# Scaling the first branch's operands later in ScalarE's order, and three gate tiles in the merge for one pair of weights

## The chip, the cores and the metric

The kernel runs on one core of a Trainium2 chip. The metric is the time of one execution on the device, in microseconds (us). The core has a matrix engine, TensorE (PE in the profile, with its weight loads as PEld), and three engines for elementwise work: VectorE (DVE), ScalarE (ACT) and GpSimd (POOL). SyncE (SP) issues nearly all DMA transfers. Each engine works off its own list of instructions in order and waits on semaphores for the others.

## The reference

One layer of a decoder in float32: S = 1024 positions, D = 1024, a hidden width of 4096.

```
h = rms_norm(x)
[A | B | C | nsa_gates | G0 G1 G2] = h @ W_in
y_0 = subln(diff_attention(A))            # 4 heads of 128, 512 columns
y_1 = sliding_window_attention(B)         # 8 heads of 64, window 128, sinks
y_2 = native_sparse_attention(C)          # compressed + selected + window 512
x = x + (sum_n sigmoid(G_n) * (y_n @ P_n)) @ W_out
x = x + relu(rms_norm(x) @ W_up)**2 @ W_down
```

`subln` is an RMS norm of each head's output with a gain per channel. P_n is 512 x 1024. The last step of the first line that matters here, the merge, is the sum over the three branches n.

## The kernel before

Every float32 operand of a product is kept as a high part and a remainder, `hi` and `lo`, and a product is three matmuls (`mm3`, L118 to L120: hi by hi, hi by lo, lo by hi). Making such a pair (`split`, L90 and L91) is a copy on ScalarE and a subtraction on VectorE or GpSimd. Activations are held transposed: channels on the 128 partitions, positions along the free axis, in two halves of 512 positions.

The order of TensorE's work is written out by hand. `mix` interleaves an attention stage (fine-grained steps) with a stage of plain products, its `dense` partner, so that TensorE has products to run while the softmax goes through the other engines. The order on the other engines is set at build time by a scheduler that goes by a timeline of its own, so a change in the code may move instructions on them in ways that the diff does not show. SP's transfers are issued in one order too.

The stages that matter:

- **Branch C, second half** (about 900 to 1172 us). The partner of the attention is `first_branch`. It runs over two halves of the positions. For each it projects some of the 24 merge gates (`gates(n)`; the sigmoid, L1125, goes to DRAM, `gd`), then scales the four operands of branch 0 (`scaled`), then makes the eight products of branch 0 and multiplies each by its gate (L1183). The products go to DRAM (`yd`).
- **One scaled operand**: a box `tm` of the tag "tm" (two buffers) receives branch A's output and its row of norms (L1141, L1142), GpSimd multiplies the two in place (L1145), ScalarE writes the high part `xh` times the gain (L1146), VectorE the remainder `xl` (L1147). The two buffers of the tag also hold the gates of branch 0, so the third operand's loads wait for the first operand's `xl`. `parts.pop(0)()` issues these three instructions between two steps of a gate's projection.
- **Attention on the other engines** in that stage: L715 makes scores `sc`, VectorE adds the bias and takes the row maximum `mc` (L739), ScalarE takes the exponential with the row sum (`expo`, L747), VectorE multiplies by one over the sum (L1048), TensorE transposes (`tr`, L763), ScalarE and VectorE split the transposed `p` into `ph` and `pl` (L90, L91) with GpSimd zeroing the rest of the tiles (L760, L761), and L903 and L904 accumulate `ac`; L909 and L910 take it out (`ot`, `ob`).
- **The merge** (`merge_and_mlp`, 1172 to about 1272 us). Branch 1 has eight weights and two halves, sixteen products; branch 2 has two halves and eight weights each, sixteen products. A product is twelve matmuls into one of six PSUM banks. VectorE makes g = (g + 1) x product (L1218 in branch 1, L1229 in branch 2). In branch 1 GpSimd adds g to y, which was read from `yd` (L1216, L1220). In branch 2 VectorE adds it (L1231), and the sum is split into `mh` and `ml` (L1232, L1233). A gate tile `g` is filled by a DMA from `gd` (L1154) and is free once it has been added; the pool `bg` has two of them. The weights' pairs `wh`, `wl` are taken from two pools in turn (`parts`), three pairs in each.
- After it come W_out (`wo`, L1285) and the MLP.

`GATES` divides the 24 gate projections among the stages; entries 3 and 4 are the gates before and during the scaling of the first half, entry 5 those before the scaling of the second half, and what remains of 24 those during it.

Of the kernel before, what the change touches and what calls it, by code (L numbers as in the profile page):

```python
# [13 lines left out]
AF = mybir.ActivationFunctionType  # L14
# [50 lines left out]


PACE = (1.6, 1.4144, 1.156, 1.392, 1.45, 1.7)
GATES = (2, 2, 12, 1, 4, 2)
STEP = ((1.702, 0.1048), (2.2511, 0.078), (1.85, 0.078))
DIST = 2  # L70
WR = 4
# [4 lines left out]
class Kernel:  # L76
# [27 lines left out]
    def parts(self, pool=None, bufs=None, tag="w"):  # L104
        pool = pool or self.wp
        if self.other is not None:
            self.turn += 1
            pool = self.other if self.turn % 2 else pool
        return [pool.tile([P, self.w_n], F32R, name=tag + x, tag=tag + x, bufs=bufs or self.w_bufs) for x in "hl"]

    def spare(self, k):
# [62 lines left out]
    def run(self):  # L174
# [70 lines left out]
        with tc.tile_pool(name="cp", side="right", **kw) as cp:  # L245
# [7 lines left out]
            self.mm = mm2  # L253
            self.mix(self.compress(cp, z, w1), self.gates(GATES[0]), PACE[5])
        self.alone = False
# [15 lines left out]
        self.load_bias(range(8, 12))  # L271
        self.mix(self.pipeline(self.items_b(1, st_b1), last=True), self.gates(GATES[1]), PACE[2])
        self.at.release()
# [15 lines left out]
        for g in range(2):  # L289
# [7 lines left out]
            if g == 0:  # L297
                dense = self.gates(GATES[2])
            else:
# [444 lines left out]
        return self.at.tile([P, n], F32, name="p", tag=f"p{kind}{qb % 2}", bufs=2)  # L744

    def expo(self, p, ps, m, l):
        self.nc.scalar.activation(p, ps, AF.Exp, bias=m, scale=-1.0, accum_out=l)  # L747

    def pblocks(self, blocks):

# [384 lines left out]
    def scaled(self, i, s, hi, lo):  # L1135

        nc = self.nc
        box = self.sq.tile([P, self.tm_n], F32, name="tm", tag="tm", bufs=2)
        raw, r = box[:, 0:512], box[:, 512:1024]
        row = self.rd[i]  # L1140
        nc.sync.dma_start(raw, self.od[i, :, s])  # L1141
        nc.sync.dma_start(r, bass.AP(tensor=row.tensor, offset=row.offset + s.start, ap=[[0, P], [1, 512]]))  # L1142

        def parts():
            nc.gpsimd.tensor_tensor(raw, raw, r, op=ALU.mult)  # L1145
            nc.scalar.activation(hi, raw, AF.Copy, scale=self.subln)  # L1146
            nc.vector.scalar_tensor_tensor(lo, raw, self.subln, hi.bitcast(F32), op0=ALU.mult, op1=ALU.subtract)  # L1147

        return parts
# [15 lines left out]
    def first_branch(self):  # L1165
        nc = self.nc
        for half, n, m in ((0, GATES[3], GATES[4]), (1, GATES[5], 24 - sum(GATES))):
            s = slice(half * 512, half * 512 + 512)
            yield from self.gates(n)
            o = [self.parts(tag="x") for _ in range(4)]  # L1170
            parts = [self.scaled(i, s, *o[i]) for i in range(2)]
            for k, c in enumerate(self.gates(m)):
                if k % 4 == 3 and parts:
                    parts.pop(0)()
                    if k < 8:
                        parts.append(self.scaled(2 + k // 4, s, *o[2 + k // 4]))
                yield c
            for d in range(KT):
                w = self.weight(self.a["wbr"][0, d], 512)
                g = self.gate(self.sq, "tm", 2, 0, d, s)  # L1180
                ps = self.branch(0, d, [x[0] for x in o], [x[1] for x in o], w)
                with self.tc.high_priority(offset=self.urgent):
                    nc.vector.scalar_tensor_tensor(g, g, 1.0, ps, op0=ALU.add, op1=ALU.mult)  # L1183
                nc.sync.dma_start(self.yd[d, :, s], g)
                yield 2.6

    def merge_and_mlp(self):
        tc, nc, a = self.tc, self.nc, self.a
        kw = dict(bufs=1, reuse_waits="tile")
        halves = [slice(0, 512), slice(512, 1024)]  # L1190
        mp = tc.alloc_tile_pool(name="mp", side="left", **kw)
        mh = mp.tile([P, KT, S], F32R, name="mh")
        ml = mp.tile([P, KT, S], F32R, name="ml")
        pre = tc.alloc_tile_pool(name="pre", side="right", **kw)
        self.wp = pre
        self.w_n, self.wr_bufs, self.w_bufs = 512, 3, 3
        with (tc.tile_pool(name="bb", side="right", **kw) as bb, tc.tile_pool(name="br", side="right", **kw) as br,
              tc.tile_pool(name="bl", side="left", **kw) as bl, tc.tile_pool(name="bg", side="left", **kw) as bg,
              tc.tile_pool(name="wx", side="left", **kw) as wx):
            self.other = wx  # L1200
            ob = [[bb.tile([P, S], F32R, name=f"ob{i}{x}") for x in range(2)] for i in range(4)]
            oc = [None, None]
            y = [None, None]
            for half, pool in ((0, br), (1, bl)):
                y[half] = pool.tile([P, KT, 512], F32, name="y")
                oc[half] = [[pool.tile([P, 512], F32R, name=f"oc{i}{x}") for x in range(2)] for i in range(4)]
            for s in halves:
                for i in range(4):
                    self.operand(self.od[4 + i], s, *[x[:, s] for x in ob[i]])
            for d in range(KT):  # L1210
                w = self.weight(a["wbr"][1, d], 512)
                if d == 1:
                    self.wo_after = self.last_load
                for half, s in enumerate(halves):
                    g = self.gate(bg, "g", 2, 1, d, s)
                    nc.sync.dma_start(y[half][:, d], self.yd[d, :, s])  # L1216
                    ps = self.branch(1, d, [x[0][:, s] for x in ob], [x[1][:, s] for x in ob], w)
                    nc.vector.scalar_tensor_tensor(g, g, 1.0, ps, op0=ALU.add, op1=ALU.mult)  # L1218
                    v = y[half][:, d, :]
                    nc.gpsimd.tensor_tensor(v, v, g, op=ALU.add)  # L1220
            for half, s in enumerate(halves):
                for i in range(4):
                    self.operand(self.od[8 + i], s, *oc[half][i])
            for half, s in enumerate(halves):
                for d in range(KT):
                    w = self.weight(a["wbr"][2, d], 512)
                    g = self.gate(bg, "g", 2, 2, d, s)
                    ps = self.branch(2, d, [x[0] for x in oc[half]], [x[1] for x in oc[half]], w)
                    nc.vector.scalar_tensor_tensor(g, g, 1.0, ps, op0=ALU.add, op1=ALU.mult)  # L1229
                    v = y[half][:, d, :]  # L1230
                    nc.vector.tensor_tensor(v, v, g, op=ALU.add)  # L1231
                    nc.scalar.activation(mh[:, d, s], v, AF.Copy, scale=0.5)  # L1232
                    nc.vector.scalar_tensor_tensor(ml[:, d, s], v, 0.5, mh[:, d, s].bitcast(F32),  # L1233
                                                   op0=ALU.mult, op1=ALU.subtract)

        self.tail(mp, mh, ml, halves, pre)
# [373 lines left out]
```

## Time and profile before

| quantity | value |
|---|---|
| time of the runs (3), median | 2022.37 us (2022.16 to 2026.12) |
| the profiled execution | 2024.17 us |
| its span | 2022.4 us |
| mean granted clock of TensorE | 0.982 |
| instructions of the scaled operands (POOL, ACT, DVE) | 8 each, 911.3 to 1050.7 us |
| DMA | 221.59 MB, mean 110 GB/s |

The profile describes one execution; its span runs from the first to the last instruction, and the execution's own time holds 1.8 us more. "Busy" is the share of the span in which an engine executes something. A row of the timeline has the start, the duration, the engine, the line and the operation, out<-in by the names of the program, and at its end in brackets how long its engine had stood idle before and what released it. The granted clock is the share of full speed at which TensorE ran.

### The profile page before, as it was taken

To read this page: it belongs to the slowest core of one execution; us is meant where nothing else is said; L and a number is where in the kernel's file an instruction comes from. 1 tells how busy PE (TensorE), PEld (TensorE's weight loads), DVE (VectorE), ACT (ScalarE), POOL (GpSimd) and SP (SyncE) were. 2 spreads that over 40 slices of the span, in tenths; PEclk is the share of its full clock that TensorE was granted. 3 is DMA by queue.
4 is the path that set the end of the run, shared out by engine and by line. 5 is a ranking of instruction groups with operands and counts; after the bars stand their busy time and mean duration, and the time that the engine had idled before them with its cause. 6 is when DMAs were issued, how large, how long until landed. Compare 5 with 4: busy or idle time off the path is not lost. (4 is left out here: it accounts for less than half of the span.)

```text
span 2022.4 us, 30612 instructions
## 1 busy us (share of the span) xinstructions
PE 1889.4 (93%) x9842; PEld 1618.3 (80%) x9842; DVE 1410.4 (70%) x3216; ACT 1006.0 (50%) x2550; POOL 953.8 (47%) x1138
## 2 busy tenths in 40 slices
PE   7999999998899999998989798998999998999998
PEld 6888889887688888877878686786788886888876
DVE  6747877788667677567676835648655544889898
ACT  5356555666445555445555623325454554433431
POOL 4455444643361212262232246218444545789783
PEclk9999999999999999999999998999999999999998
DMA  6132012101211111213243475425544446445343
GB/s 221 51 105 56 12 53 54 52 16 56 81 42 47 57 58 52 72 42 97 84 139 100 137 238 186 142 83 182 177 158 154 161 137 240 140 157 162 120 146 115
DMA packets 123773, 221.59 MB, mean 110 GB/s; under 512 B 14580, under 2 KB 35604, under 8 KB 123612
## 3 DMA queue, kind: packets, MB, share of 16 engines
q1 hardware_dynamic: 122028, 213.87, 32.7%
q10 hardware_dynamic: 1584, 5.77, 0.8%
q8 instruction: 78, 1.28, 0.3%
q14 instruction: 83, 0.68, 0.1%
HBM read 158.68 MB, written 64.83 MB: 111 GB/s over the span
## 5 line engine op out<-in xcount | busy, mean ns | idle before, releaser
L91 POOL TENSOR_TENSOR wl<-wr,wh 128x512 fp32r<-128x512 f32 (+3 forms) x246 | 325.6, 1330 | 273.9 <-ACT wh L90 231.2
L90 ACT ACTIVATE wh<-wr 128x512 fp32r<-128x512 f32 (+3 forms) x258 | 150.3, 590 | 185.7 <-PE mm L119 114.9
L715 PE MATMUL sc<-st 128*128 128x256 f32 (+5 forms) x736 | 182.3, 342 | 24.3 <-ACT p L747 24.0
L90 ACT ACTIVATE ph<-tr 128x384 fp32r<-128x384 f32 (+3 forms) x280 | 138.4, 497 | 116.2 <-PE tr L763 96.1
L91 DVE TENSOR_TENSOR pl<-tr,ph 128x384 fp32r<-128x384 f32 (+3 forms) x280 | 155.6, 559 | 43.6 <-ACT ph L90 41.5
L760 POOL MEMSET ph<- 128x128 f32 x152 | 34.7, 228 | 269.4 <-PE ac L903 220.8
L118 PE MATMUL mm<-hh,wh 128*128 128x512 f32 x384 | 159.4, 415 | 0.0
L715 PEld LDWEIGHTS sc<-st 128*128 128x128 f32 x736 | 122.3, 191 | 44.9 <-ACT p L747 36.0
L120 PE MATMUL mm<-hh,wl 128*128 128x512 f32 x384 | 152.1, 396 | 0.0
L119 PE MATMUL mm<-hl,wh 128*128 128x512 f32 x384 | 152.0, 396 | 0.0
L119 PE MATMUL mm<-wl,wh 128*128 128x512 f32 x352 | 140.3, 398 | 9.0 <-POOL wl L91 9.0
L118 PE MATMUL mm<-wh 128*128 128x512 f32 x352 | 140.4, 399 | 8.1 <-DVE x L1492 5.2
L90 ACT ACTIVATE wh<-u 128x512 fp32r<-128x512 f32 x162 | 93.1, 620 | 106.4 <-PE mm L119 27.9
L120 PE MATMUL mm<-wh,wl 128*128 128x512 f32 x352 | 139.5, 396 | 0.0
L763 PE MATMUL tr<-ident,p 128*128 128x128 f32 x792 | 129.9, 277 | 9.3 <-DVE st L568 8.3
L747 ACT ACTIVATE p<-sc,mc 128x256 f32<-128x256 f32 (+5 forms) x200 | 106.7, 539 | 46.8 <-DVE mc L739 43.5
L903 PE MATMUL ac<-ph,st 128*128 128x256 f32 x392 | 110.2, 299 | 20.4 <-DVE ob L910 13.7
L91 POOL TENSOR_TENSOR wl<-s,wh 128x512 fp32r<-128x512 f32 x64 | 89.1, 1399 | 78.9 <-ACT wh L90 78.9
L118 PE MATMUL mm<-wh,hh 128*128 128x384 f32 (+1 forms) x320 | 116.3, 364 | 0.6 <-ACT raw L524 0.6
L91 DVE TENSOR_TENSOR wl<-u,wh 128x512 fp32r<-128x512 f32 x98 | 113.5, 1159 | 3.6 <-ACT wh L90 3.6
L904 PE MATMUL ac<-pl,st 128*128 128x256 f32 x392 | 106.3, 291 | 7.4 <-DVE pl L91 6.7
L119 PE MATMUL mm<-wl,hh 128*128 128x384 f32 (+1 forms) x320 | 109.7, 343 | 0.0
(312 smaller groups left out, 5714.0 us busy)
## 6 DMA issues: line engine op xcount, KB each, us to landing
ud<-u SPq DMA_DIRECT2D x112, 256.0 KB, 2.1
u<-ud SPq DMA_DIRECT2D x98, 256.0 KB, 3.6
wr<-wu SPq DMA_DIRECT2D x76, 256.0 KB, 3.0
wr<-wd SPq DMA_DIRECT2D x64, 256.0 KB, 3.0
gd<-go SPq DMA_DIRECT2D x48, 256.0 KB, 2.0
g<-gd SPq DMA_DIRECT2D x48, 256.0 KB, 3.3
wr<-wg SPq DMA_DIRECT2D x40, 256.0 KB, 2.7
wr<-wbr SPq DMA_DIRECT2D x40, 256.0 KB, 3.4
```

The source lines that it names most:

```text
L90: nc.scalar.activation(hi, src, AF.Copy)
L91: (eng or nc.vector).tensor_tensor(lo, src, hi.bitcast(F32), op=ALU.subtract)
L118: mm(out, lh, rh, start=first, stop=False, skip_group_check=more)
L119: mm(out, lh, rl, start=False, stop=False, skip_group_check=more)
L120: mm(out, ll, rh, start=False, stop=last, skip_group_check=more)
L715: self.nc.tensor.matmul(ps[:, off:off + k1 - k0], q[:, t * P:(t + 1) * P], k[:, k0:k1], start=i == 0, stop=i == 1)
L747: self.nc.scalar.activation(p, ps, AF.Exp, bias=m, scale=-1.0, accum_out=l)
L760: nc.gpsimd.memset(ph[0:rows, o:o + P].bitcast(F32), 0.0)
L763: nc.tensor.transpose(pt[0:rows, o:o + P], src, self.ident)
L903: nc.tensor.matmul(ac, v, ph, start=first, stop=False)
L904: nc.tensor.matmul(ac, v, pl, start=False, stop=last)
```

## The change

There are five edits.

1. `GATES`: of the five gates that go with the scaling of the first half, two instead of one are projected ahead of it and three instead of four during it; of the three of the second half, one instead of two ahead and two instead of one during it. The totals stay.
2. In `first_branch` an operand is scaled every `gap` steps, with gap = min(4 m, 8) = 8 for both halves, where it was every 4.
3. `expo` keeps the last exponential that was issued, and `scaled` puts ScalarE's copy behind it in ScalarE's order (`issue_after`).
4. The merge's gate tiles are three instead of two, for branch 1 and for branch 2.
5. The second of the two pools of weight pairs in the merge holds two pairs instead of three.

```
-GATES = (2, 2, 12, 1, 4, 2)
+GATES = (2, 2, 12, 2, 3, 1)
...
             pool = self.other if self.turn % 2 else pool
+            bufs = bufs or (2 if pool is self.other else None)
...
     def expo(self, p, ps, m, l):
-        self.nc.scalar.activation(p, ps, AF.Exp, bias=m, scale=-1.0, accum_out=l)
+        self.last_exp = self.nc.scalar.activation(p, ps, AF.Exp, bias=m, scale=-1.0, accum_out=l).ins
...
             nc.gpsimd.tensor_tensor(raw, raw, r, op=ALU.mult)
-            nc.scalar.activation(hi, raw, AF.Copy, scale=self.subln)
+            with self.tc.issue_after(self.last_exp):
+                nc.scalar.activation(hi, raw, AF.Copy, scale=self.subln)
...
+            gap = min(4 * m, 8)
             for k, c in enumerate(self.gates(m)):
-                if k % 4 == 3 and parts:
+                if k % gap == gap - 1 and parts:
                     parts.pop(0)()
-                    if k < 8:
-                        parts.append(self.scaled(2 + k // 4, s, *o[2 + k // 4]))
+                    if k < 2 * gap:
+                        parts.append(self.scaled(2 + k // gap, s, *o[2 + k // gap]))
...
-                    g = self.gate(bg, "g", 2, 1, d, s)
+                    g = self.gate(bg, "g", 3, 1, d, s)
...
-                    g = self.gate(bg, "g", 2, 2, d, s)
+                    g = self.gate(bg, "g", 3, 2, d, s)
```

TensorE's order is the same, instruction for instruction. Line numbers behind L746 are 1 to 3 higher in the changed kernel (L747 is L748, L1146 is L1148, L1154 is L1156, L1216 is L1219).

ScalarE in the first half of `first_branch`, before: the third and fourth copy `xh` among the exponentials `p` of one block of the attention.

```order
L1146 ACTIVATE xh_11378<-tm_11450,subln_212 128x512
L90 ACTIVATE wh_11852<-wr_11851 128x512
L747 ACTIVATE p_11551,lc_11534<-sc_11536,mc_11535 128x448
L747 ACTIVATE p_11551,lc_11534<-sc_11545,mc_11535 128x320
L747 ACTIVATE p_11586,lc_11534<-sc_11570,mc_11535 128x384
L747 ACTIVATE p_11586,lc_11534<-sc_11582,mc_11535 128x256
L1146 ACTIVATE xh_11380<-tm_11506,subln_212 128x512
```

The first and second copy in the changed kernel, some 20 us of the program further on:

```order
L748 ACTIVATE p_11703,lc_11638<-sc_11699,mc_11639 128x256
L1148 ACTIVATE xh_11608<-tm_11616,subln_212 128x512
L1126 ACTIVATE go_11742<-mm_11634 128x512
L90 ACTIVATE ph_11733<-tr_11735 128x512
L90 ACTIVATE ph_11774<-tr_11776 128x384
L748 ACTIVATE p_11764,lc_11749<-sc_11751,mc_11750 128x512
L748 ACTIVATE p_11764,lc_11749<-sc_11758,mc_11750 128x512
L748 ACTIVATE pc3_7133,lc_11749<-sc_11784,mc_11750 128x64
L90 ACTIVATE wh_12147<-wr_12146 128x512
L90 ACTIVATE ph_11804<-tr_11806 128x384
L748 ACTIVATE p_11818,lc_11749<-sc_11784,mc_11750 128x384
L748 ACTIVATE p_11818,lc_11749<-sc_11814,mc_11750 128x256
```

The copies have gone from ahead of a block's exponentials to behind the last of a block; what stood behind the copies of before now has nothing of the kind ahead of it.

VectorE in the second half, before: the fourth and last remainder `xl`, ahead of the row sums `lc` and the attention's output `ob`.

```order
L739 ISA sc_12980,mc_12952<-sc_12980,bias_10690,mc_12952 128x256
L739 ISA mc_12952 128x1
L1147 SCALAR_TENSOR_TENSOR xl_13362<-tm_13475,subln_212,xh_13361 128x512
L1044 TENSOR_TENSOR lc_12951<-lc_12951 128x1
L1045 RECIPROCAL lc_12951<-lc_12951 128x3
L1046 TENSOR_TENSOR lc_12951<-lc_12951,cgate_224 128x3
L910 TENSOR_TENSOR ob_13007<-ac_12779,ot_13006 64x256
```

In the changed kernel the last remainder of that half stands some 54 us of the program later, behind the scaling of the `p` of another block (L1049) and just ahead of the merge's first operands `ob`:

```order
L1046 RECIPROCAL lc_13589<-lc_13589 128x3
L1047 TENSOR_TENSOR lc_13589<-lc_13589,cgate_224 128x3
L1049 TENSOR_SCALAR pc1_7131<-pc1_7131,lc_13589 128x64
L1049 TENSOR_SCALAR p_13597<-p_13597,lc_13589 128x256
L1049 TENSOR_SCALAR p_13636<-p_13636,lc_13589 128x256
L1149 SCALAR_TENSOR_TENSOR xl_13143<-tm_13369,subln_212,xh_13142 128x512
```

SP at the merge's start, before: the loads of `y` and of the first gates `g`.

```order
L911 DMA od<-ob 64x256 x2
L1154 DMA g<-gd 128x512 x2
L911 DMA od<-ob 64x256
L1216 DMA y<-yd 128x512 x12
L1154 DMA g<-gd 128x512
L1216 DMA y<-yd 128x512 x4
L1154 DMA g<-gd 128x512
```

In the changed kernel:

```order
L912 DMA od<-ob 64x256 x2
L1156 DMA g<-gd 128x512 x2
L912 DMA od<-ob 64x256
L1219 DMA y<-yd 128x512
L1156 DMA g<-gd 128x512
L1219 DMA y<-yd 128x512 x10
L1156 DMA g<-gd 128x512
L1219 DMA y<-yd 128x512 x4
L1156 DMA g<-gd 128x512
```

The third gate's load has moved ahead of eleven loads of `y`; the later ones each wait for the tile of three gates before instead of two.

## The prediction

> **What bounds the kernel now.** I read the page first, for the share of each engine, then TensorE's timeline for its idle time, then the table of windows around what I found, since an average over this program says little.
>
> ```profile
> span 2022.4 us, 30612 instructions
> PE 1889.4 (93%) x9842; PEld 1618.3 (80%) x9842; DVE 1410.4 (70%) x3216; ACT 1006.0 (50%) x2550; POOL 953.8 (47%) x1138
> ```
>
> TensorE (PE) is busy 93% and its order of work is written out by hand and isn't touched, so the change can only move the 7% in which it stands and the time in which its clock is low. In the windows table a row is stretch, length, then busy time of PE, PEld, DVE, ACT and POOL, then granted clock, DMA share and GB/s:
>
> ```profile
> 925.00:930.00 5.00, 3.41 (x9) 2.83 (x10) 2.61 (x11) 3.01 (x10) 2.54 (x2) 0.60 0.38 114
> 930.00:935.00 5.00, 5.00 (x25) 4.29 (x25) 2.43 (x5) 2.20 (x4) 1.56 (x3) 0.72 0.22 57
> 1030.00:1040.00 10.00, 7.94 (x49) 6.91 (x48) 6.05 (x17) 4.16 (x12) 3.15 (x6) 0.93 0.53 166
> 1040.00:1050.00 10.00, 9.57 (x48) 8.27 (x48) 7.79 (x26) 4.67 (x14) 4.11 (x5) 0.90 0.38 126
> 1172.62:1227.16 54.54, 54.54 (x240) 45.16 (x241) 20.76 (x25) 13.47 (x22) 32.06 (x25) 1.00 0.74 248
> 1227.16:1271.78 44.62, 37.44 (x145) 29.95 (x144) 29.91 (x38) 15.46 (x28) 23.29 (x17) 0.89 0.58 188
> ```
>
> The first four rows are branch C's second half, where the first branch's operands are scaled; the last two are the merge. The stalls of PE in them, with what released it in brackets:
>
> ```profile
> 914.47 0.50 PE L715 MATMUL sc<-st 128*128 128x256 f32 x2 [0.91 <-ACT p L747]
> 926.59 0.79 PE L715 MATMUL sc<-st 128*128 128x256 f32 x2 [3.77 <-ACT p L747]
> 1036.04 0.38 PE L903 MATMUL ac<-ph,st 128*128 128x256 f32 x1 [0.96 <-ACT ph L90]
> 1037.53 0.38 PE L904 MATMUL ac<-pl,st 128*128 128x256 f32 x1 [1.10 <-DVE pl L91]
> 1046.04 0.51 PE L715 MATMUL sc<-st 128*128 128x256 f32 x2 [0.43 <-ACT p L747]
> 1053.65 0.39 PE L903 MATMUL ac<-ph,vct 128*128 128x256 f32 x1 [2.40 <-DVE ob L910]
> 1233.36 0.76 PE L118 MATMUL mm<-oc,wh 128*128 128x512 f32 x1 [3.31 <-DVE g L1218]
> 1244.46 0.77 PE L118 MATMUL mm<-oc,wh 128*128 128x512 f32 x1 [3.86 <-DVE g L1229]
> ```
>
> Each of the first six stands near one of the scaled copies; each of the last two waits for a gate's product. So both parts of the change aim at stalls that PE has.
>
> **The first branch: what goes.** The chain in front of the 3.77 us stall, from the timeline of all engines:
>
> ```profile
> 922.16 0.54 DVE L91 TENSOR_TENSOR pl<-tr,ph 128x384 fp32r<-128x384 f32 x1
> 923.81 0.72 ACT L1146 ACTIVATE xh<-tm,subln 128x512 fp32r<-128x512 f32 x1 [2.02 <-POOL tm L1145]
> 924.56 0.75 DVE L1147 SCALAR_TENSOR_TENSOR xl<-tm,subln,xh 128x512 fp32r<-128x512 f32 x1 [0.51 <-ACT xh L1146]
> 925.23 0.48 DVE L739 CUSTOM_DVE_ANT_0 sc<-sc,bias,mc 128x256 f32<-128x256 f32 x1
> 925.81 0.64 ACT L747 ACTIVATE p<-sc,mc 128x448 f32<-128x448 f32 x1 [0.76 <-DVE mc L739]
> ```
>
> ScalarE (ACT) stands 2.02 us for GpSimd's product, copies, then VectorE (DVE) takes the remainder xl, and only then the score's maximum (L739) that the exponential waits for. Without the pair, L739 can follow pl at 922.70 instead of 925.23: PE would go on 2.5 us sooner, and 1.3 us of the stall stay (score, maximum and exponential in turn). At the other five stalls one copy of 0.72 or one remainder of 0.75 to 0.99 (at 1036) stands in front; I take 0.7 of 0.91, 0.7 of 0.96, 1.0 of 1.10, 0.4 of 0.43, and 0.7 of 2.40. Sum with the 2.5: 6.0 us, between 2.5 (the first chain alone) and 9.6 (all six rows).
>
> Behind these stalls the granted clock is low: 5 x 0.40 + 5 x 0.28 = 3.4 us in the first two windows, of which up to 0.8 lies in idle time already counted (1.59 us idle at half); I take 3.0. In the next two, 10 x 0.07 + 10 x 0.10 = 1.7. If the stall shrinks below what lowers the clock, these 4.7 us go. Together 10.7 us.
>
> That the clock falls behind stalls is the trace's reading: it is 0.93 and 0.90 around 1038, after 0.96 and 1.10 us of idle, and 1.00 in the merge's window without idle. [...]
>
> **The first branch: what is paid.** The eight products, copies and remainders remain, in other places:
>
> ```profile
> L1145 POOL TENSOR_TENSOR tm<-tm x8: 1264/1286/1403, 911.3 to 1048.6; 128x512 f32<-128x512 f32 x8
> L1146 ACT ACTIVATE xh<-tm,subln x8: 714/724/727, 912.7 to 1050.0; 128x512 fp32r<-128x512 f32 x8
> L1147 DVE SCALAR_TENSOR_TENSOR xl<-tm,subln,xh x8: 737/752/1306, 913.4 to 1050.7; 128x512 fp32r<-128x512 f32 x8
> 957.41 0.39 PE L904 MATMUL ac<-pl,st 128*128 128x256 f32 x1 [1.44 <-DVE pl L91]
> 1092.33 1.23 DVE L91 TENSOR_TENSOR pl<-tr,ph 128x512 fp32r<-128x512 f32 x2 [0.35 <-POOL pl L761]
> 1093.20 0.28 PE L904 MATMUL ac<-pl,st 128*128 128x256 f32 x1
> 1104.94 0.61 DVE L1048 TENSOR_SCALAR p<-p,lc 128x256 f32<-128x256 f32 x2
> 1105.03 0.39 PE L119 MATMUL mm<-xl,wh 128*128 128x512 f32 x1
> ```
>
> ScalarE's copies now stand behind exponentials that already wait for DVE, so I price them at nothing there: ACT is busy 4.2 of 10 us in these windows; uncovered, each would be 0.72. The remainders land on DVE ahead of a pl. The one near 956.7 is ahead of the pl that PE already waits 1.44 us for: +0.75. Of the next half's, the third is ahead of the pl at 1092.33, whose first half PE takes at 1093.20, some 0.2 us after it is made: +0.55. The others meet pl's with about 1 us of slack. The last remainder of the second half stands behind the two L1048 that end at 1105.55, so it ends near 1106.30, and branch 0's matmul needs it at 1105.03: +1.27. On GpSimd (POOL) a product of 1.29 us can stand ahead of the zeroing (L760, L761) of a ph that PE waits for: 0 to 1.3, I take 0.6, half, since no row shows which comes first. Moved with the copies are two pairs of loads on SP a half (the third and fourth operand, whose box is freed by xl); they come a few us later, behind nothing that waits. The gate that moves between the halves leaves PE's order as it is. Paid: 0.75 + 0.55 + 1.27 + 0.6 = 3.2 us, between 0 and 8 x 0.75 = 6.0. The first branch nets **7.5 us**.
>
> **The merge.** What holds the products is a ring of two gate tiles:
>
> ```profile
> 1225.68 0.68 DVE L1218 SCALAR_TENSOR_TENSOR g<-g,mm 128x512 f32<-128x512 f32 x1
> 1228.11 1.29 POOL L1220 TENSOR_TENSOR y<-y,g 128x512 f32<-128x512 f32 x1
> 1229.43 0.48 SPq L1154 DMA_DIRECT2D g<-gd  x1
> 1232.52 0.69 DVE L1218 SCALAR_TENSOR_TENSOR g<-g,mm 128x512 f32<-128x512 f32 x1 [6.17 <-DMA g<-gd]
> DVE g L1218 <- DMA g<-gd: 20.7, 8, 6.2
> DVE g L1229 <- DMA g<-gd: 9.3, 6, 4.0
> ```
>
> A tile is multiplied until 1226.36, added to y until 1229.40, refilled from 1229.43, and multiplied again until 1233.21: 6.85 us a round, 3.42 us a gate with two tiles. PE makes a product in 54.54 / 20 = 2.73 us (240 matmuls, 12 a product). DVE falls behind by 0.7 us a product, and when PE's six banks are full PE stands. With three tiles a gate takes 2.28 us, less than 2.73, so DVE keeps up: the ring no longer sets the pace. In the last window 144 matmuls should take 12 x 2.73 = 32.7 us and the stretch takes 44.62: 11.9 us lost, of which the two stalls are 7.2 and the low clock (0.11 x 44.62 = 4.9) about the rest. All 11.9 go if no other wait takes their place.
>
> The tile is paid with one pair of weights: six pairs in two pools become five.
>
> ```profile
> 1178.17 0.63 ACT L90 ACTIVATE wh<-wr 128x512 fp32r<-128x512 f32 x1 [2.91 <-PE mm L119]
> 1183.61 0.63 ACT L90 ACTIVATE wh<-wr 128x512 fp32r<-128x512 f32 x1 [4.81 <-PE mm L119]
> 1278.72 0.50 PE L119 MATMUL mm<-wo,mh 128*128 128x512 f32 x1 [1.79 <-DVE wo L91]
> ```
>
> A pair of the smaller pool is now rewritten after product n-4 and needed at product n: three products, 8.2 us, for a copy of 0.63 and a remainder of about 1.3. ACT already waits 2.91 and 4.81 us for such releases while PE stands nowhere (54.54 of 54.54), so this costs between nothing and one stall like 3.86; I take 1, near the row without idle. The wait for DVE's wo at 1278.72 may shorten when DVE isn't behind: 0 to 1.79, I take 0.9. The merge nets 11.9 - 1 + 0.9 = **11.8 us**.
>
> **Sum.** 7.5 + 11.8 = 19.3 us. The profiled execution took 2024.17 us (span 2022.4 and 1.8 around it), which gives 2004.9; it is 1.8 us above the median of the runs, 2022.37, and against that the forecast is 2003.
>
> **The rivals.**
> - Merge only: the moved copies, remainders and products make as much new idle as they remove, and the clock stays low there. For it: DVE is busy 6 to 8 of 10 us in those windows. Against: it asks for 10.7 us of cost where I count 3.2. 2022.4 - 11.8 = 2010.6.
> - First branch only: with three tiles DVE's product waits for something else (POOL is busy 32 of 54.5 us in the merge and adds each y; or the five weight pairs), and PE stands as long. Against: POOL's add of 1.29 per 2.73 us. 2022.4 - 7.5 = 2014.9.
> - The low clock has another cause than these stalls and stays when they go: 4.7 us in the first branch and 4.7 in the merge less, 19.3 - 9.4 = 9.9, so 2012.5. Against: in the merge's first window, as dense as any, the clock is 1.00.
> - Nothing that PE waits for moves: the copies come later, but the exponentials were waiting for score and maximum, and the gate ring for the y loads' traffic (DMA share 0.74). Then 2022.
> - Slower: the ring of five pairs. ACT works in order; a wh copy that waits for its pair holds the mh copies behind it, and PE lacks the weights. A late pair costs about what a late gate did, 11.9 / 2 = 5.95 us with its clock. It decides from four late pairs of the eight that the small pool serves in branch 2: 4 x 5.95 = 23.8 against 19.3 gained. Five would give 2022.4 + 29.8 - 19.3 = 2033. Against: 8.2 us of lead for 1.9 of work.
>
> **How the numbers follow.** Forecast 0.56, merge only 0.11, first branch only 0.10, clock stays 0.05: these are faster, 0.82. Nothing moves: 0.10, the same. Slower: 0.08. About 0.2% (4 us) is what a measurement of this kernel can tell from no change. The forecast's own bounds are a gain of 9.6 + 4.7 and 11.9 + 1.8, nothing paid, 28 us (1994), down to 2.5 + 4.7 - 6.0 and 11.9 - 3.9, 9 us (2013). The range of 1995 to 2017 takes this in, and first branch only; it leaves out the last two cases, 0.18.
>
> **What would show it.** Right: no stall near 926 above 1.5 us, and the clock over 0.95 in 925 to 935 and 1030 to 1050; a stall of about 1.3 us at branch 0's second start; in the merge no row of PE released by L1221 or L1232 (the gates' products), the window of its last 12 products near 33 us, and DVE's waits for g below 2 us each. Wrong: a PE stall released by wh or wl in branch 2 (the ring of weights), by pl beside an xl (more than 3 us in all), or the low clock in the same places without a stall before it.

## The result, and the profile after

The changed kernel takes 2006.72 us in the median of six runs (2002.73 to 2011.69); the kernel before, over six runs, 2023.56 us (2019.25 to 2027.96). The ratio is 0.9913, with a 95% interval of 0.9897 to 0.9928: 17.6 us less, between 14.6 and 20.8. The forecast was 19.3 less. A second set of runs of the same kernel, further down, gave 0.9897 (0.9878 to 0.9915).

The profiled execution of the changed kernel took 2011.07 us, so it is one of its longer ones, 13.1 us below the profiled execution of before. The first lines of its page, as before:

```profile
span 2009.3 us, 30615 instructions
PE 1889.3 (94%) x9842; PEld 1616.0 (80%) x9842; DVE 1422.2 (71%) x3216; ACT 1006.1 (50%) x2550; POOL 959.3 (48%) x1138
```

Nothing has become cheaper: the busy times of PE and ACT are within 0.1 us of before, DVE's and POOL's are a little higher. What went is idle time and low clock. The windows table, with the same columns as in the prediction (the granted clock is third from the end):

```profile
905.00:935.00 30.00, 27.78 (x160) 23.75 (x161) 24.38 (x73) 17.91 (x52) 7.52 (x13) 1.00 0.31 99
1030.00:1050.00 20.00, 18.77 (x109) 16.15 (x108) 14.43 (x52) 11.46 (x36) 5.18 (x13) 1.00 0.17 57
1168.22:1222.76 54.54, 54.54 (x241) 45.16 (x242) 23.36 (x29) 12.82 (x22) 36.19 (x27) 1.00 0.81 269
1222.76:1261.38 38.62, 34.49 (x145) 26.49 (x144) 36.12 (x38) 18.68 (x34) 25.77 (x17) 1.00 0.67 227
```

The clock is 1.00 where it was 0.60, 0.72, 0.93 and 0.90 (first two rows) and where it was 0.89 (last row). The last row runs from the same instruction of PE to the same instruction as the last window of before: 38.62 us instead of 44.62. PE's timeline has these waits in the places that the prediction named, and two further on (1109 and 1119) that the kernel before has too:

```profile
923.93 0.50 PE L716 MATMUL sc<-st 128*128 128x256 f32 x2 [1.10 <-ACT p L748]
952.08 0.39 PE L905 MATMUL ac<-pl,st 128*128 128x256 f32 x1 [1.63 <-DVE pl L91]
1031.17 0.39 PE L904 MATMUL ac<-ph,st 128*128 128x256 f32 x1 [0.33 <-POOL ph L761]
1042.83 0.39 PE L904 MATMUL ac<-ph,vct 128*128 128x256 f32 x1 [0.81 <-DVE ob L911]
1084.02 0.38 PE L905 MATMUL ac<-pl,st 128*128 128x256 f32 x1 [1.30 <-DVE pl L91]
1097.18 0.50 PE L120 MATMUL mm<-xl,wh 128*128 128x512 f32 x1 [0.81 <-DVE xl L1149]
1109.75 0.52 PE L716 MATMUL sc<-st 128*128 128x256 f32 x2 [2.08 <-ACT p L748]
1119.69 0.38 PE L904 MATMUL ac<-ph,vct 128*128 128x256 f32 x1 [1.78 <-DVE ob L911]
1223.84 0.50 PE L121 MATMUL mm<-oc,wl 128*128 128x512 f32 x1 [0.47 <-POOL wl L91]
1230.63 0.50 PE L121 MATMUL mm<-oc,wl 128*128 128x512 f32 x1 [1.01 <-POOL wl L91]
```

The 3.77 us stall is 1.10, those near 914, 1036, 1037 and 1046 are gone, and 2.40 is 0.81. Of the two long stalls behind gates none is left. New are the waits for GpSimd's zeroing (1031), for a pl (1084) and for the last operand (1097), all three foreseen, and the waits for the weights' remainders wl: the waits table of 1165 to 1275 gives their sum, and the gates':

```profile
DVE g L1221 <- DMA g<-gd: 12.5, 5, 4.0
PE mm L121 <- POOL wl L91: 4.1, 5, 1.3
DVE g L1232 <- DMA g<-gd: 0.7, 1, 0.7
```

Since PE's instructions are the same in every kernel of this study, in the same order, each can be compared by the start of the same instruction in two timelines. The table gives, for stretches between fixed instructions of PE (named by their start before), how much longer or shorter than in the profile of before each profiled execution was, in us.

| kernel | to 880 | 880 to 1020 | 1020 to 1095 | 1095 to 1172.6 | 1172.6 to 1227 | 1227 to 1272 | 1272 to 1300 | whole PE |
|---|---|---|---|---|---|---|---|---|
| the change | +0.8 | -6.1 | -3.8 | +4.7 | 0.0 | -6.0 | -2.1 | -13.2 |
| the change, second set | -4.3 | -6.6 | -3.5 | +4.5 | +1.6 | -10.3 | -2.1 | -19.5 |
| fb_only | -4.5 | -6.5 | -3.2 | +6.5 | +1.2 | -2.1 | +2.1 | -5.8 |
| merge_only | -8.5 | -2.1 | +2.2 | +0.4 | 0.0 | -7.4 | -2.1 | -17.8 |
| no_issue_after | -5.9 | -2.3 | +2.0 | +0.7 | 0.0 | -7.2 | -2.1 | -13.6 |
| gates2_pairs5 | -7.2 | -6.5 | -2.6 | +5.2 | 0.0 | -2.1 | +1.9 | -10.6 |
| no_gap | -2.2 | -2.7 | -2.9 | +7.9 | +1.6 | -7.7 | -2.1 | -6.5 |
| gap_8_6 | -5.6 | -4.0 | -3.5 | +4.9 | +1.6 | -10.2 | -2.1 | -17.8 |
| wo_later | -1.9 | -6.5 | -2.9 | +3.6 | 0.0 | -6.2 | -2.1 | -15.1 |
| wo_spread | -5.2 | -4.1 | -2.8 | +5.2 | +1.6 | -8.8 | -2.1 | -15.2 |
| wo_spread_early | -4.3 | -3.9 | -2.6 | -0.5 | 0.0 | -6.5 | -2.1 | -20.7 |
| gates3_pairs6 | -7.8 | -4.0 | -3.6 | +5.9 | +1.6 | -6.0 | +16.7 | +5.0 |
| ob_later | -4.4 | -6.7 | -3.2 | +9.1 | 0.0 | -6.8 | -2.1 | -11.9 |

The first column is a warning: no edit touches that part, and it differs by up to 9 us between executions. So a single "whole" of this table says little, and verdicts below go by the ratios of the runs; the stages are read where the change is. The column 1095 to 1172.6 holds a loss that the prediction did not have.

### The profile page after: what moved, and what is told of

The parts are those of the page before. It is cut to its first block, busy times and chain, and to the rows that moved or that the text cites. A ratio compares the mean times of both kernels' runs of the same rounds, so it can differ in the third digit from the quotient of the medians.

```text
span 2009.3 us, 30615 instructions
## 1 busy us (share of the span) xinstructions
PE 1889.3 (94%) x9842; PEld 1616.0 (80%) x9842; DVE 1422.2 (71%) x3216; ACT 1006.1 (50%) x2550; POOL 959.3 (48%) x1138
## 5 line engine op out<-in xcount | busy, mean ns | idle before, releaser
L764 PE MATMUL tr<-ident,p 128*128 128x128 f32 x792 | 129.8, 277 | 8.5 <-DVE st L569 7.0
L748 ACT ACTIVATE p<-sc,mc 128x256 f32<-128x256 f32 (+5 forms) x200 | 106.7, 539 | 50.8 <-DVE mc L740 47.5
```

The source lines that it names most:

```text
L748: self.last_exp = self.nc.scalar.activation(p, ps, AF.Exp, bias=m, scale=-1.0, accum_out=l).ins
L764: nc.tensor.transpose(pt[0:rows, o:o + P], src, self.ident)
```

## The experiments

All times are ratios to the kernel before, measured beside it on the same chip, with 95% intervals. fb_only, merge_only, no_issue_after and gates2_pairs5 share a chip; so do gates3_pairs6, gap_8_6, wo_later and no_gap; and so do whole_again, wo_spread and wo_spread_early. Kernels that share none are compared by their ratios.

### The two parts, and their pieces

`fb_only` takes back edits 4 and 5:

```
-            bufs = bufs or (2 if pool is self.other else None)
...
-                    g = self.gate(bg, "g", 3, 1, d, s)
+                    g = self.gate(bg, "g", 2, 1, d, s)
```

(and the same for branch 2.)

> The first branch's part alone (edits 1 to 3; two gate tiles and six weight pairs as before). If the two parts add up: in the profile the stalls and the low clock of 912 to 1054 gone as with the whole change (about 12 us earlier at 1053), then some 3 us given back at a pl near 1093 and at the last xl; the merge with its two stalls of 3.3 and 3.9 us and their clock; in all 4 to 10 us faster than before. Rival, the gain comes from the merge alone: within 3 us of before. Rival, the parts need each other: slower than before.

Measured: 0.9954 (0.9937 to 0.9970), 9.3 us less. The merge has its stalls as before, both somewhat shorter:

```profile
1226.55 0.70 PE L119 MATMUL mm<-oc,wh 128*128 128x512 f32 x1 [2.62 <-DVE g L1221]
1237.37 0.77 PE L119 MATMUL mm<-oc,wh 128*128 128x512 f32 x1 [3.50 <-DVE g L1232]
```

The gain stands without the merge's part. More than 3 us are given back in 1095 to 1172.6, though: +6.5 in the table.

`merge_only` is the kernel before with edits 4 and 5 alone.

> The merge's part alone (edits 4 and 5). If the parts add up: the first branch as before with its 3.77 us stall, the merge without stalls behind g, with five short ones behind wl of 4 us together, 7 to 10 us faster than before. Together with the first branch's part alone it should make the 17 us of the whole. Rival, the merge's gain hangs on the phase in which the first branch leaves the other engines: stalls behind g come back, within 3 us of before.

Measured: 0.9947 (0.9928 to 0.9966), 10.7 us less, no stall behind g, four waits behind wl of 3.0 us together. The two parts make 9.3 + 10.7 = 20.0 us; the whole makes 17.6 in its first set and 20.8 (0.9897) in its second. They add up within their intervals. Up to 1120 us of its own time the other engines of this kernel run what they ran before, in the same order, so its -2.1 and +2.2 in the table's stretches from 880 to 1095 show how much one execution differs from another there.

`no_issue_after` is the whole change without edit 3:

```
-            with self.tc.issue_after(self.last_exp):
-                nc.scalar.activation(hi, raw, AF.Copy, scale=self.subln)
+            nc.scalar.activation(hi, raw, AF.Copy, scale=self.subln)
```

> The whole change without edit 3: copies wherever the scheduler puts them, which is near their places of before, four in a row of exponentials in each half. If the rule that puts a copy behind an exponential is what removes the stall at 926: a stall of over 3 us there and low clock behind it, low clock near 1038 too, the time that of the merge's part alone, 5 to 10 us slower than the whole change. Rival, the gates and the wider gap do it: within 3 us of the whole change.

Measured: 0.9945 (0.9924 to 0.9966), as the merge's part alone. The stall is back:

```profile
919.64 0.58 PE L716 MATMUL sc<-st 128*128 128x256 f32 x1 [2.87 <-ACT p L748]
```

So edits 1 and 2 do nothing without edit 3: up to 1122 us the order on VectorE, ScalarE and GpSimd, copies included, is that of the kernel before.

`no_gap` is the whole change without edits 1 and 2 (`GATES` as before, `gap = 4`).

> The whole change without edits 1 and 2: gates and spacing as before, the copies behind the last exponential only. Two copies of the first half then stay within the block of the 3.77 us stall, each behind an exponential. If order behind the exponential alone is what counts: the stall near 926 shrinks below 1.5 us. If the distance counts too: a stall of 1.5 to 3.5 us stays there, and the time lies between the merge's part alone and the whole change, 2 to 5 us above the latter.

Measured: 0.9936 (0.9918 to 0.9954), 5 to 8 us above the whole change by the ratios of its two sets; the interval overlaps that of the first set and lies just above that of the second. Behind the exponentials, but too close together, the copies of the first half still make most of the long stall:

```profile
923.00 0.50 PE L716 MATMUL sc<-st 128*128 128x256 f32 x2 [3.25 <-ACT p L748]
```

The copies of the second half, though, stand some 45 us later than before, and the stalls near 914, 1036, 1037 and 1046 are gone here as well. So the long stall needs order and distance; for the four others the order alone was enough.

`gates2_pairs5` is the whole change with two gate tiles again (edit 4 undone, edit 5 kept).

> The whole change without edit 4: two gate tiles and five pairs of weights. If the ring of gate tiles makes the merge's long stalls: two stalls behind g of 3 to 4 us with low clock behind them, as before, and the merge 6 to 12 us longer than with three tiles. If the missing pair makes the short stalls behind wl: they stay. Rival, the earlier third gate load and the order on SP do it, not the ring: no stall behind g.

Measured: 0.9950 (0.9933 to 0.9967), the same as fb_only. Both long stalls are back in PE's timeline, and in the windows table, below it, the clock of the last twelve products is 0.92:

```profile
1222.08 0.72 PE L119 MATMUL mm<-oc,wh 128*128 128x512 f32 x1 [2.97 <-DVE g L1221]
1232.35 0.74 PE L119 MATMUL mm<-oc,wh 128*128 128x512 f32 x1 [2.91 <-DVE g L1232]
```

```profile
1215.97:1258.54 42.57, 36.69 (x145) 29.11 (x144) 29.81 (x37) 15.92 (x29) 25.78 (x18) 0.92 0.61 204
```

The ring of gate tiles made the stalls. The missing pair costs nothing here: 42.57 us against 42.56 in fb_only with six pairs, and no wait behind wl. By what I had expected, this speaks against the missing pair as the maker of the short waits behind wl; but the stalls behind the gates also leave the remainders more time. The waits show only once the gates no longer hold PE back.

### Why a pair was given up

`gates3_pairs6` is the whole change without edit 5: three gate tiles and six pairs.

> The whole change without edit 5: three gate tiles and all six pairs of weights. In SP's order all eight loads of W_out then stand behind the last weight of branch 2, since their buffers lie where the second pool of weights ends. If the pair was given up for that room: no short stall behind wl in branch 2, but PE waits for wo at W_out's first products, 10 us or more with low clock behind, and the time is above that of the whole change by 8 us or more. Rival, the ring of five pairs is what costs (the short stalls, 5.4 us): then this is up to 5 us faster than the whole change.

Measured: 1.0021 (1.0007 to 1.0035), 22 us slower than the whole change by the ratios, the largest effect of the study. Branch 2 runs without a wait, and then W_out waits for its own operands, four times:

```profile
1256.80 0.80 PE L119 MATMUL mm<-wo,mh 128*128 128x512 f32 x1 [4.66 <-ACT wo L90]
1263.77 0.80 PE L119 MATMUL mm<-wo,mh 128*128 128x512 f32 x1 [2.62 <-ACT wo L90]
1270.57 0.80 PE L119 MATMUL mm<-wo,mh 128*128 128x512 f32 x1 [2.45 <-ACT wo L90]
1277.28 0.80 PE L119 MATMUL mm<-wo,mh 128*128 128x512 f32 x1 [2.35 <-ACT wo L90]
```

The same place in the windows table:

```profile
1255.50:1282.90 27.40, 15.93 (x28) 7.95 (x29) 9.10 (x10) 9.71 (x17) 10.02 (x8) 0.50 0.50 171
```

The clock is 0.50 throughout. In SP's rows the first loads of W_out (`x<-wo`) stand behind the last weights, first this kernel, then the changed one:

```profile
1251.74 0.90 SPq L1288 DMA_DIRECT2D x<-wo  x2
```

```profile
1182.00 1.01 SPq L1288 DMA_DIRECT2D x<-wo  x2
```

This is what the theory of the room said: with the pair, the loads of W_out find no place before the last weights are used up.

### The waits behind wl

In the changed kernel's timeline of GpSimd, two halves of a row of W_out stand ahead of the remainders that PE waits for at 1223.84 and 1230.63 (an entry with x2 is two instructions):

```profile
1218.64 3.45 POOL L91 TENSOR_TENSOR wo<-x,wo 128x512 fp32r<-128x512 f32 x2
1222.05 3.44 POOL L91 TENSOR_TENSOR wl<-wr,wh 128x512 fp32r<-128x512 f32 x2
1225.45 3.44 POOL L91 TENSOR_TENSOR wo<-x,wo 128x512 fp32r<-128x512 f32 x2
1228.87 1.71 POOL L91 TENSOR_TENSOR wl<-wr,wh 128x512 fp32r<-128x512 f32 x1
```

A third of the five waits (1256.22, 0.91 us) has two such halves ahead of it as well. The other two have another chain. Ahead of the longest (1243.24, 1.27 us) GpSimd stood idle until ScalarE had made a copy `wh`, and ScalarE had waited for that weight's load:

```profile
1239.51 0.63 ACT L90 ACTIVATE wh<-wr 128x512 fp32r<-128x512 f32 x1 [2.39 <-DMA wr<-wbr]
1240.22 2.97 POOL L91 TENSOR_TENSOR wl<-wr,wh 128x512 fp32r<-128x512 f32 x2 [5.64 <-ACT wh L90]
```

GpSimd waits for a copy `wh` ahead of the one at 1249.43 (0.47 us) too. Whether the smaller ring of pairs has a part in these two is not shown: gates3_pairs6 has six pairs and none of the waits, but there W_out's loads and splits come later too.

`wo_later` holds GpSimd's splits of W_out back behind the remainder of branch 2's seventh weight:

```
...
+                with tc.issue_after(self.wl_after if k % 2 == 0 else self.wo_after):
+                    self.split(wo[k][0][:, s], wo[k][1][:, s], r[:, s], nc.vector if k % 2 else nc.gpsimd)
...
```

> The whole change with GpSimd's splits of W_out held back behind the weight of branch 2's seventh product (first half). If these splits make the first short stalls behind wl (0.47 and 1.01 us near 1224 and 1231): those two are gone, and a later one may grow, as two W_out rows are then split back to back (6.9 us); net 0 to 2 us faster in the merge. Rival, the ring of five pairs makes them: they stay.

Measured: 0.9914 (0.9894 to 0.9934), no difference to the whole change. The first two waits are gone, and behind four halves in a row (6.85 us) there is one as long as several:

```profile
1224.51 6.85 POOL L91 TENSOR_TENSOR wo<-x,wo 128x512 fp32r<-128x512 f32 x4
1231.32 3.38 POOL L91 TENSOR_TENSOR wl<-wr,wh 128x512 fp32r<-128x512 f32 x2
1234.76 0.50 PE L121 MATMUL mm<-oc,wl 128*128 128x512 f32 x1 [3.92 <-POOL wl L91]
```

So the first two waits move with W_out's splits. Two kernels spread them; both also have the second half's operands every 6 steps:

```
-            gap = min(4 * m, 8)
+            gap = 8 if half == 0 else 6
...
+                with tc.issue_after(self.los[min(6 + k + i, 15)] if k % 2 == 0 else self.wo_after):
...
```

(`los` are the remainders of branch 2 in order; i is the half of the row; `wo_spread_early` begins at 3 instead of 6.)

> The whole change with the second half's operands every 6 steps, and GpSimd's splits of W_out put one by one between the weights of branch 2 (a remainder wl, half a row of W_out, a remainder, and so on, from the sixth product on). If two W_out halves in a row in front of the weights are what makes PE wait for wl: the waits of 4 to 5 us in the merge fall below 1.5 us and the time is 2 to 5 us under that of the whole change. Rival, GpSimd has too much to do in branch 2 whatever its order: the waits come later, the sum stays near 4 us.

> The same with the halves of W_out spread from where they stand now on (the first right behind the last y). By the first theory half of the waits remain, 2 us; by the rival, 4 us as before.

> The whole change as it is, beside the two below on one chip: 0.985 to 0.995 of before, the merge's five short stalls behind wl again, the stall near 924 at 1.1 us, and low clock somewhere in 1100 to 1125.

Measured, on one chip: whole_again 0.9897 (0.9878 to 0.9915), wo_spread 0.9896 (0.9874 to 0.9918), wo_spread_early 0.9910 (0.9890 to 0.9930). No difference that can be told. wo_spread has two waits behind wl of 0.91 and 1.06 us, wo_spread_early two behind wl of 1.0 together and one of 1.66 behind wh, but whole_again itself has a single long one of 0.91 where the first profile of the same kernel had five: this missed what I had expected of it. The waits vary from one execution to the next more than the edits move them, so these runs show nothing to win here.

### The loss between 1095 and 1172

`gap_8_6` changes only the spacing of the second half (the first edit of the fence above).

> The whole change with the second half's operands scaled every 6 steps instead of 8, so that the last remainder stands some 27 rows earlier on VectorE, ahead of neither the branch's first product nor a pl. If the late last operand is what gives back the first branch's gain: no stall behind xl near 1097 (0.81 us), none behind pl near 1084 (1.30), and less of the low clock of 1107 to 1124, 3 to 8 us faster than the whole change. Rival, that low clock comes from the ob splits and the maxima alone, whatever the operands do: only 1 to 3 us faster. Second rival, the operands meet other rows and cost the same there: within 1 us.

Measured: 0.9906 (0.9889 to 0.9924), within 2 us of the whole change. There is no wait for xl any more, but the wait for the pl stays (1.46 us where 1.30 should have gone), and so do the stalls further on and the low clock behind them (+4.9 in the table; from 1106.84 to 1110.41 a matmul of 128x512 takes 0.63 us, where it is 0.39 at full clock):

```profile
1104.94 0.51 PE L716 MATMUL sc<-st 128*128 128x256 f32 x2 [2.25 <-ACT p L748]
1113.11 0.39 PE L904 MATMUL ac<-ph,vct 128*128 128x256 f32 x1 [1.22 <-DVE ob L911]
1120.53 0.80 PE L716 MATMUL sc<-st 128*128 128x256 f32 x2 [2.17 <-ACT p L748]
```

The late last operand is not the cause. At that place ScalarE copies branch 1's operands for the merge, and waits for their loads with exponentials behind it (the changed kernel's second set):

```profile
1101.55 0.63 ACT L90 ACTIVATE ob<-wr 128x512 fp32r<-128x512 f32 x1 [1.55 <-DMA wr<-od]
1103.84 0.63 ACT L90 ACTIVATE ob<-wr 128x512 fp32r<-128x512 f32 x1 [1.36 <-DMA wr<-od]
1105.08 0.64 PE L716 MATMUL sc<-st 128*128 128x256 f32 x2 [2.46 <-ACT p L748]
```

`ob_later` puts each of the eight copies behind a later exponential, two exponentials apart:

```
-                    self.operand(self.od[4 + i], s, *[x[:, s] for x in ob[i]])
+                    with tc.issue_after(self.exps[2 * (i + 4 * (s.start > 0)) - 26]):
+                        self.operand(self.od[4 + i], s, *[x[:, s] for x in ob[i]])
```

> The whole change with ScalarE's eight copies of branch 1's operands (ob, L90) each held behind a later exponential, the first behind those that PE waits for near 1105. If these copies, which wait for their loads ahead of the exponentials, and their remainders among the maxima make the stalls of 1104 to 1115 (0.5 to 3 us each), and these the low clock: the stalls near 1105 fall below 1 us, the low clock of 1105 to 1125 is gone, the stretch between the first product of branch 0's second half and the merge is 4 to 8 us shorter, and the time 3 to 8 us under that of the whole change. Rival, the attention's own chain makes them: the stalls stay within 0.5 us of 2.4. Second rival, the copies now stand ahead of later exponentials and cost the same there: within 2 us.

Measured: 0.9933 (0.9912 to 0.9954), 4 to 7 us above the whole change by the ratios of its two sets, with intervals that overlap. The stall at 1105 is gone, so these copies made it. One behind it is new (1122), three are longer than in the changed kernel's first profile (1108, 1141, 1154), and there is more low clock (+9.1; four transposes of L764 take 1.05 us near 1137, 1142, 1155, 1157 and 1159, where others take 0.60):

```profile
1108.79 0.39 PE L904 MATMUL ac<-ph,vct 128*128 128x256 f32 x1 [2.24 <-DVE ob L911]
1122.35 0.39 PE L904 MATMUL ac<-ph,vct 128*128 128x256 f32 x1 [2.05 <-DVE ob L911]
1141.27 0.79 PE L716 MATMUL sc<-st 128*128 128x256 f32 x2 [2.94 <-ACT p L748]
1154.30 0.47 PE L764 MATMUL tr<-ident,pc 128*128 128x128 f32 x1 [2.56 <-DVE pc L1049]
```

The second rival of that run comes nearest, but it had the time within 2 us, and three of the four stalls are released by VectorE: that the moved copies make them is not shown. No version of this study beats the changed kernel by more than can be measured.

## Why the prediction was right, step by step

**The first branch, what goes.** Forecast: 6.0 us of idle time and 4.7 of low clock, with 1.3 left of the 3.77 us stall. Measured: 0.91, 3.77 - 1.10, 0.96, 1.10, 0.43 and 2.40 - 0.81, together 7.7 us of idle, and the low clock gone entirely in both places. At these places it was right, and a little small. That it is edit 3 that does it is shown by no_issue_after, and that the long stall needs edits 1 and 2 as well by no_gap.

**The first branch, what is paid.** Forecast 3.2. Measured in the changed kernel: the pl near 957 +0.19 (forecast 0.75), a pl near 1093 1.30 (0.55), the last xl 0.81 (1.27), GpSimd's zeroing 0.33 (0.6), behind a product of 1.29 us and a remainder: 2.6 us of idle. Right in kind at the last three places. Of the pl near 957 one profile can't tell: in the second set it is 1.21 us, less than the 1.44 of before.

**What was missed in the same part.** The stretch from 1095 to 1172.6 is 4.7 us longer, and only 0.8 of that is the operand's wait. The prediction asked what is late next after each stall that goes, but only next to the copies; it did not ask it of the stalls that lay further on and that PE already had, as this one of the kernel before:

```profile
1117.31 0.50 PE L715 MATMUL sc<-st 128*128 128x256 f32 x2 [1.87 <-ACT p L747]
```

This stall is 2.08 to 2.80 us long in eight of the ten profiles that have edit 3 and branch 1's copies in their old place, 1.87 to 2.33 in the three without edit 3; and behind it, in nine of the ten, stands low clock that those three do not have (0.50 over 6.83 us from 1110.10 in the changed kernel's first profile, 1.00 from 1113.71 to 1120.54 in that of before and from 1105.56 to 1112.40 in merge_only). Nine of the ten lose 3.6 to 7.9 us there, the two others without edit 3 lose 0.4 and 0.7. What makes this stall is shown: branch 1's operands. Why the low clock comes with the change is not settled: it is not the last operand (gap_8_6), and the idle time of PE in that stretch is 11.9 us before and after. By the counts of the last section the stall is long enough to cost clock in the kernels without edit 3 too, where it falls into one window. My estimate from their three traces: a window of 3.41 us laid at random has PE busy under 45% there with chances of 47, 66 and 75%, against 67 to 83% in the nine that lost clock. That all three escaped would be luck of about 1 in 20, so neither the change nor luck is shown to be the cause.

**The merge.** Forecast: 11.9 us of stalls and low clock go, 0.9 at W_out, 1 is paid to the ring of weights. The stalls are gone and the clock is 1.00; at W_out 2.1 us are gone, more than the bound of 1.79. But the step that the five pairs cost 1 us, "between nothing and one stall like 3.86", failed in its mechanism, and its size was off too: by the starts of the same instructions, the five waits cost 0.7 to 1.5 us each, 5.4 together, in the profile of the first set. The prediction's own sign of being wrong, a PE stall released by wl in branch 2, did appear. The prediction looked for a copy that waits for its pair. What the rows show is GpSimd with W_out's splits ahead of the remainders for three of the waits (wo_later moved two of them) and a late copy wh for the other two; a part of the ring in these is not excluded. The window of the last twelve products is 38.62 us instead of the 33 that I named (44.62 - 11.9), 34.28 in the second set. The forecast that DVE's waits for g stay below 2 us holds for branch 2 (0.7) and not for branch 1 (4.0), where they hold nobody up: PE is busy 54.54 of 54.54 us there.

**The sum.** 7.5 + 11.8 = 19.3 was forecast; the parts alone give 9.3 and 10.7, the whole 17.6 and 20.8. In the profiles the first branch is worth less than by the runs: from 880 to 1172.6 us the changed kernel is 5.2 us shorter than before, 5.6 in the second set, and fb_only 3.2. In that stretch PE's waits (those over 0.15 us) fell from 27.2 to 21.4 us, but half clock cost 6.8 us before and costs 6.8 us in the changed kernel's first profile: it left the copies' places and came back further on. So "these 4.7 us go" holds at the two places and not for the stage; more idle time went than forecast, and that the number came out so near is partly luck. Whether fb_only's 9.3 us (6.1 to 12.8 by its interval) or the 3.2 of its one profile is nearer to the worth of the first branch stays open.

**The rivals.** Merge only (2010.6) and first branch only (2014.9) are excluded by the two kernels that hold one part each. That the low clock stays in its places is excluded by the windows; that as much of it comes back elsewhere none of the rivals had. Slower through the ring of five pairs is excluded by the result; the opposite was near: without giving up the pair the change would have been 0.2% slower than before.

**The clock.** The prediction took from the trace of before that the clock falls behind stalls, and counted 1.7 us of low clock near 1040 (0.93 and 0.90) to the stalls of 0.96 and 1.10 us there. With those stalls the low clock is gone (1.00 in 1030 to 1050), so this reading held; the last section has the numbers.

## What to carry to other kernels

An elementwise copy that waits for another engine cost little by itself here (0.72 us) and much by what stood behind it on its own engine (a stall of PE of 3.77 us): put it behind the last thing that the bottleneck waits for, and look whether the next such copy is far enough behind it, since here the longest stall went only with order and distance together. A ring of tiles is sized by its round trip over its tiles against the consumer's pace (6.85 us over 2 against 2.73, over 3 below it), and the room for one more tile is best taken where the ring has slack; where it was not taken, the next stage's prefetch lost 17 us. A stall cost twice where the matrix engine's clock dropped with it: the one of 3.77 us has 6.83 us at a clock of 0.50 from 925.98 on, 3.4 us of full speed. So stalls that are borderline by the counts below are worth a look even far from the edit.

## What the runs showed of the hardware

In the profile of before and in that of the changed kernel TensorE's granted clock is 1.00 or 0.50, and all its changes lie a whole number of windows of 3.41 us apart (to 0.01 us). It dropped behind windows in which PE was partly busy, not only behind idle ones. Two such windows, each with the one that follows, first of the kernel before, then of the changed one:

```profile
1035.21:1038.62 3.41, 1.48 (x10) 1.28 (x11) 3.01 (x9) 2.29 (x8) 1.40 (x5) 1.00 0.45 149
1038.62:1042.04 3.42, 3.42 (x17) 3.33 (x17) 1.66 (x4) 1.47 (x3) 0.85 (x1) 0.50 0.78 240
```

```profile
1106.69:1110.10 3.41, 1.32 (x10) 1.03 (x9) 2.63 (x9) 2.63 (x7) 0.00 (x0) 1.00 0.99 347
1110.10:1113.52 3.42, 2.86 (x8) 2.15 (x7) 3.22 (x7) 2.28 (x8) 3.23 (x3) 0.50 0.80 249
```

PE was busy 1.48 of 3.41 us (43%) and 1.32 (39%), and the window behind has half the clock. And the same place of the program in the kernel before, where the windows lay otherwise (the stall ends 3.60 us behind a window's start, 1117.31 against 1113.71; in the changed kernel 3.06, 1109.75 against 1106.69):

```profile
1113.71:1117.13 3.42, 1.73 (x12) 1.37 (x10) 3.40 (x12) 2.47 (x7) 0.00 (x0) 1.00 0.79 277
1117.13:1120.54 3.41, 2.65 (x11) 2.10 (x12) 3.21 (x10) 2.82 (x10) 1.80 (x2) 1.00 0.84 281
```

Busy 1.73 of 3.42 (51%): the clock stays. Counted over these two profiles, from 21 us on, where their records of the clock begin: 22 of the 23 windows at full clock in which PE was busy under 45% were followed by half clock; 8 of 23 between 45 and 61%; and none of 1082 above. All 10 windows at half clock in which it was busy under 80% were followed by another, and 2 of 30 above. In gates3_pairs6 the clock was 0.50 over 27.40 us in which PE was busy 15.93 us (58%). Low clock is 3.41, 6.83 or 10.24 us long in both profiles, except where the program's end cuts it off: one to three windows, each 1.7 us of full speed.

The part before 880 us, the same in all kernels, took up to 8.5 us less than in the profile of before. Before has five windows of half clock there, 8.5 us of full speed together; the changed kernel has seven, at +0.8 us. That the place of the windows against the program makes a part of this spread is my estimate. Further on, no low clock stands behind the stall of 1.87 us in the kernel before, and behind that of 2.08 us in the changed one 6.83 us of it, 3.4 us of full speed: more than the stall itself.
